# A two-layer encoder in float32: output projections and w_down by token instead of by feature

## Chip, cores and metric

One core of a Trainium2 chip. The metric is device time of one execution in microseconds (us). The kernel before takes 2138.07 us, the median of 3 runs (2137.47 to 2138.16).

## What is computed

256 tokens of 2048 features go through two pre-norm layers, in float32. Layer 0 has chunked attention in 8 heads beside differential attention in 4; layer 1 has an index-selected sparse attention in 16 heads over a shared latent. What matters here is the frame around the heads:

```python
for layer in range(DEPTH):                       # DEPTH = 2
    h = rmsnorm(x, attn_norm[layer])
    p = h @ w_in                                 # even_w_in or odd_w_in
    mix = heads(p) @ w_out                       # even_w_out or odd_w_out, 2048 x 2048
    x = x + mix
    h = rmsnorm(x, ffn_norm[layer])
    x = x + (silu(h @ w_gate[layer]) * (h @ w_up[layer])) @ w_down[layer]   # 5632 x 2048
return rmsnorm(x, final_norm)
```

## The kernel before

**Numbers.** Every large product is made of three: operands are split into a high part in a reduced float32 form (F32R) and a remainder (low), and high x high, high x low and low x high are summed in PSUM. Activations live as `[feature, high/low, token]` tiles: `xs` (normalised input, 16 tiles of 128 features), `mix` (heads' output), `y` (FFN's inner activations, 44 tiles).

**Weights.** All weights are streamed once, in an order that the generator `sources` (L97) sets, in pieces of 256 input features by 512 outputs, laid out as 128 x 1024. `load_w` (L120) issues a piece's DMA on SyncE's queue (SP) into one of 5 buffers `wl`, ScalarE (ACT) writes the high part `wh` and VectorE (DVE) the remainder `wo`, 3 buffers each. `next_w` (L139) keeps up to three pieces loaded ahead in program order.

**Two forms of product.** `gemm_t` (L187) gives outputs by feature: the weight is the stationary operand, 128 outputs at a time, and the tokens stream. Per piece and 128 outputs it issues two matmuls of `wh` with high and low tokens side by side, 512 columns, and two of `wo` with the high tokens, 256 columns; 16 matmuls per piece into four PSUM banks `acc0` to `acc3`, whose two halves still have to be added. `gemm_n` (L222) gives outputs by token: a block of 128 tokens is stationary, and 512 weight columns stream; per piece 12 matmuls of 512 columns into two banks `nat0` and `nat1`. Only value projections and `w_uv` use `gemm_n`; everything else, output projections (`out_proj`, L576) and `w_down` (`ffn_layer`, L617) among it, uses `gemm_t`.

**Order around the change.** Python code issues instructions in program order, and a tile framework places semaphores and buffers. While a product runs, `pump` (L150) advances a queue of generators, `steps`, twice per piece: norm statistics, attention scores and mixes are slipped between matmuls that way. `drain` empties the queue.

**Residual and norms.** The residual `xt` is kept by feature, `[128, 16, 256]`. A product's 512 outputs are one of four groups. After each group `add_residual` (L307) adds both halves of four banks to `xt` (`add_tiles`, 8 adds on DVE), writes the next `xs` with the norm's gain (`normalize_tiles`, ACT and DVE) and squares on ACT (`add_squares`), which GpSimd (POOL) sums in `sqacc`. The norm itself is a factor per token: `norm_steps` (L273) sums `sqacc` over partitions by matmuls with ones (`col_sums`), takes the power -1/2 on POOL (`rstd`), and spreads it over partitions with two more matmuls (`rows_of`); products are scaled after the fact.

**The end.** The last group of the last `w_down` holds two pieces back (`last=2`) and finishes its four tiles one after another (`finish_tile`, L638). Then come the sums over partitions, the power, the row, nine steps of scaling on DVE and nine stores of `out_T` (L813 to L825).

`fp.tile([P, 88])`, and `attention_pools(stack, 8)` and `(stack, 168)`, allocate spacers: unused floats in front of `y` and `mix`.

Of the kernel before, what the change touches and what calls it, by code (L numbers as in the profile page):

```python
# [39 lines left out]
def encoder_kernel(  # L40
    ctx: ExitStack,
    tc: tile.TileContext,
    xT: bass.AP,
    gcols: bass.AP,
# [15 lines left out]
    outT: bass.AP,  # L60
# [10 lines left out]
    xt = const.tile([P, KT, S], F32, name="xt")  # L71
# [11 lines left out]

    OUT0 = [4, 5, 6, 7, 0, 1, 2, 3]
# [11 lines left out]

    def sources():  # L97
        for quad in QUADS:
            for g in even_groups(quad):
                yield from (w_ein[g, k] for k in range(KT // 2))  # L100
        for g in range(4):
            yield from (w_eout[g, k] for k in OUT0)
        yield from ffn_sources(0)
        yield from (w_ox[k] for k in range(KT // 2))
        yield from (w_oi[k] for k in range(KT // 2))
        for quad in range(4):
            yield from (w_oq[quad, k] for k in range(KT // 2) if quad)
            yield w_uk[quad]
            yield w_uv[quad]
# [10 lines left out]
    def load_w(cuts=1, between=None):  # L120
        src = next(stream, None)
        if src is None:
            return
        if before:
# [62 lines left out]
    def gemm_t(act, nk, order=None, last=0, done=None, halves=0):  # L187

        banks = [bank([P, 2, S], f"acc{i}") for i in range(4)]
        order = list(range(nk // 2)) if order is None else order  # L190

        def tile_products(n, i, w, js=(0, 1)):
            cs = [slice(j * 512 + n * P, j * 512 + (n + 1) * P) for j in js]
            products(banks[n], P, w, cs, [act[:, 2 * order[i] + j] for j in js],
                     i == 0 and js[0] == 0, i == len(order) - 1)

        for i in range(len(order) - last):
            w = next_w()
            for js in ((0,), (1,)) if i < halves else ((0, 1),):
                for n in range(4):  # L200
                    tile_products(n, i, w, js)
                    if n % 2 and js[-1]:
                        pump()
        if last:
            ws = [next_w() for _ in range(last)]
            done(3, banks[3], False)
            banks.append(bank([P, 2, S], "acc4"))
            for n in range(4):
                for i, (wh, wo) in enumerate(ws):
                    ii = len(order) - last + i  # L210
                    if n < 3:
                        tile_products(n, ii, (wh, wo))
                    else:
                        for j in range(2):
                            c = slice(j * 512 + n * P, j * 512 + (n + 1) * P)
                            a = act[:, 2 * order[ii] + j]
                            mm3(banks[4][:, 0, :], (wh[:, c], wo[:, c]), (a[:, 0, :], a[:, 1, :]),
                                i == 0 and j == 0, i == last - 1 and j == 1)
                done(n, banks[n if n < 3 else 4], True)
        return banks  # L220

    def gemm_n(lhs, nk):  # L222

        banks = [bank([P, 512], f"nat{i}") for i in range(2)]
        for k2 in range(nk // 2):
            wh, wo = next_w()
            for b in range(2):
                for j in range(2):
                    h, l = lhs(2 * k2 + j)
                    t = slice(b * P, (b + 1) * P)  # L230
                    c = slice(j * 512, (j + 1) * 512)
                    mm3(banks[b], (h[:, t], l[:, t]), (wh[:, c], wo[:, c]),
                        k2 == 0 and j == 0, k2 == nk // 2 - 1 and j == 1)
                pump()
        return banks

    def xpair(kt):
        return xs[:, kt, 0, :], xs[:, kt, 1, :]
# [9 lines left out]
    def rstd(total, n, name):  # L248
        v = small.tile([P, 2], F32, name=name + "v", tag="rv", bufs=3)
        nc.vector.tensor_scalar(out=v, in0=total, scalar1=1.0 / n, scalar2=EPS, op0=ALU.mult, op1=ALU.add)  # L250
        r = small.tile([P, 2], F32, name=name + "r", tag="rc", bufs=4)
        nc.gpsimd.tensor_tensor(out=r, in0=v, in1=mhalf, op=ALU.pow)
        return r

    def col_sums(parts, name):
# [5 lines left out]
        return p[:, 0:2]  # L261

# [21 lines left out]
    def normalize_tiles(t0, n, gi):  # L284

        for t in range(t0, t0 + n):
            g = gc[:, gi * KT + t:gi * KT + t + 1]
            nc.scalar.activation(xs[:, t, 0, :], xt[:, t, :], AF.Copy, scale=g)
            nc.vector.scalar_tensor_tensor(out=xs[:, t, 1, :], in0=xt[:, t, :], scalar=g,
                                           in1=xs[:, t, 0, :].bitcast(F32), op0=ALU.mult, op1=ALU.subtract)  # L290

    def add_squares(st, t0, n):
        sq = small.tile([P, 2, S], F32, name="sq", tag="sq")
        nc.scalar.activation(sq[:, :n, :], xt[:, t0:t0 + n, :], AF.Square)  # L294
        if st["acc"] is None:
            st["acc"] = const.tile([P, 2, S], F32, name="sqacc", tag="sqacc")
            nc.gpsimd.tensor_copy(out=st["acc"], in_=sq)
        else:
            nc.gpsimd.tensor_tensor(out=st["acc"][:, :n, :], in0=st["acc"][:, :n, :], in1=sq[:, :n, :], op=ALU.add)  # L299

    def add_tiles(banks, t0):

        for i, b in enumerate(banks):
            for part in range(2):
                nc.vector.tensor_tensor(out=xt[:, t0 + i, :], in0=b[:, part, :], in1=xt[:, t0 + i, :], op=ALU.add)  # L305

    def add_residual(banks, t0, gi, st):  # L307

        for h in range(0, 4, 2):
            add_tiles(banks[h:h + 2], t0 + h)  # L310
            normalize_tiles(t0 + h, 2, gi)
            add_squares(st, t0 + h, 2)
# [6 lines left out]


    nc.scalar.dma_start(out=xt[:, 0:1, :], in_=xT[:, 0:1, :])
# [12 lines left out]
    def load_x(t, n):  # L334
        if t:
            nc.sync.dma_start(out=xt[:, t:t + n, :], in_=xT[:, t:t + n, :])
        normalize_tiles(t, n, 0)
# [8 lines left out]

    def attention_pools(stack, spacer):
        ap = stack.enter_context(tc.tile_pool(name="attn", bufs=2))
        mixp = stack.enter_context(tc.tile_pool(name="mix", bufs=1))
        mixp.tile([P, spacer], F32, name="spacer")  # L350
        return ap, mixp, mixp.tile([P, KT, 2, S], F32R, name="mix")
# [134 lines left out]
    stack = ExitStack()  # L486
    ap, mixp, mix = attention_pools(stack, 8)
# [45 lines left out]
    n0 = {"acc": None}  # L533

    def stat_steps():
        for t in range(0, KT, 2):
            with tc.issue_after(latest["act"].ins):
                add_squares(n0, t, 2)
            yield
        yield from norm_steps(n0, "n0", scale, 4)  # L540

    steps.append(bias_steps())
    for quad in QUADS:
# [21 lines left out]
        vb = gemm_n(xpair, KT)  # L565
# [10 lines left out]
    def out_proj(mix, order, gi):  # L576
        st = {"acc": None}
        for g in range(4):
            banks = gemm_t(mix, KT, order)
            if g == 0:  # L580
                drain()
            add_residual(banks, 4 * g, gi, st)
# [6 lines left out]
    def ffn(st):  # L589

        with tc.tile_pool(name="ffn", bufs=1) as fp:
            fp.tile([P, 88], F32, name="spacer")
# [22 lines left out]
            yield y  # L615

    def ffn_layer(st, gi, last):  # L617
        out = {"acc": None}
        body = ffn(st)
        y = next(body)  # L620
        for g in range(4):
            fin = last and g == 3
            banks = gemm_t(y, FT, last=2 if fin else 0, done=finish_tile(out) if fin else None)
            if fin:
                pass
            elif last:
                for h in range(0, 4, 2):
                    t = 4 * g + h
                    add_tiles(banks[h:h + 2], t)
                    add_squares(out, t, 2)  # L630
                    times_gain(t, 2)
            else:
                add_residual(banks, 4 * g, gi, out)
# [4 lines left out]
    def finish_tile(out):  # L638
        def done(n, b, fin):

            t = 12 + n
            for part in range(1 if n == 3 and fin else 2):
                nc.vector.tensor_tensor(out=xt[:, t, :], in0=b[:, part, :], in1=xt[:, t, :], op=ALU.add)
            if not fin:
                return
            if n < 3:
                add_squares(out, t, 1)
            else:
                sq = small.tile([P, 2, S], F32, name="sq", tag="sq")
                nc.scalar.activation(sq[:, 0, :], xt[:, t, :], AF.Square)  # L650
                out[n] = sq[:, 0, :]
            if n < 2:
                times_gain(t, 1)
        return done

    def times_gain(t0, n):
        for t in range(t0, t0 + n):
            nc.scalar.activation(xt[:, t, :], xt[:, t, :], AF.Copy, scale=gc[:, 64 + t:65 + t])
# [6 lines left out]
    ap, mixp, mix = attention_pools(stack, 168)  # L665
# [144 lines left out]
    out = ffn_layer(st, 4, True)  # L810


    r = rstd(col_sums([out["acc"][:, 1, :], out["acc"][:, 0, :], out[3]], "n4cs"), D, "n4")  # L813
    p = rows_of(r, "n4p")
    t = 0
    for n in (1, 1, 2, 2, 2, 2, 2, 2, 2):
        if t + n < KT:
# [69 lines left out]
```

## Time and profile before

| | |
|---|---|
| median of 3 runs | 2138.07 us |
| the profiled execution | 2138.02 us |
| its span (first to last instruction) | 2136.2 us |
| PE busy | 2122.6 us, 12280 matmul records |
| DVE, ACT, POOL busy | 1347.7, 1067.7, 231.0 us |
| moved by DMA | 398.92 MB, mean 187 GB/s |

The span is what the profile's views divide up; 1.8 us of the execution lie outside it. PE is TensorE's matmul queue, PEld its weight loads. A matmul's recorded end is modelled and overlaps the next one, so what a matmul costs is read from the distance between starts. float32 matmuls (with `ident` or `ones`) leave two records each, transposes one.

### The profile page before, as it was taken

Reading aid. Unit: us, or ns where it says so; the run is one execution under the profiler, and the core shown is the slowest. Engines: PE = TensorE matmul, PEld = TensorE weight load, DVE = VectorE, ACT = ScalarE, POOL = GpSimd, SP = SyncE. Lnnn points to the kernel's source line nnn. Section 1 sums busy time; section 2 is a strip of 40 time slices with the busy share of each in tenths; the row PEclk is TensorE's granted clock in tenths of the full one; section 3 lists DMA queues with packets and bytes.
Section 4 is the critical chain, followed back from the end, with each engine's and each line's share of the span. In section 5 each row is a group of like instructions: output and inputs, shape, how many; then the busy total and the mean of one; then the engine's idle time right before and its main releaser. Section 6 shows DMA issues by size and latency. Waiting matters only on the chain.

```text
span 2136.2 us, 31865 instructions
## 1 busy us (share of the span) xinstructions
PE 2122.6 (99%) x12280; PEld 1862.8 (87%) x12280; DVE 1347.7 (63%) x1978; ACT 1067.7 (50%) x1575; POOL 231.0 (11%) x232
## 2 busy tenths in 40 slices
PE   9999999999999999999999999999999999999998
PEld 8888888888888888888888888888888888888887
DVE  6665557766666666655547977666666666654444
ACT  6555555545454544444435566454454545444442
POOL 3111001100000000000002242110010000100000
PEclk9999999999999999999999999999999999999999
DMA  8455445555555555555556444655555555555553
GB/s 288 163 179 177 168 168 187 189 195 188 190 193 190 190 194 188 192 192 187 180 185 214 164 160 147 198 188 190 195 188 192 192 189 193 191 189 193 191 190 127
DMA packets 114407, 398.92 MB, mean 187 GB/s; under 512 B 12554, under 2 KB 16718, under 8 KB 114254
## 3 DMA queue, kind: packets, MB, share of 16 engines
q1 hardware_dynamic: 114110, 396.75, 56.0%
q8 instruction: 96, 1.57, 0.3%
q14 instruction: 57, 0.47, 0.1%
q10 hardware_dynamic: 144, 0.13, 0.0%
HBM read 394.70 MB, written 2.14 MB: 186 GB/s over the span
## 4 chain that ended last, share of the span: by engine, by line
PE 95%; DVE 2%; POOL 1%; ACT 1%; issue 1%; DMA 1%; SPq 0%; POOLq 0%; DVEq 0%; ACTq 0%
PE acc L171 86%; PE nat L171 4%; PE x L171 1%; DVE wo L136 1%; DMA xt<-in_xT 1%; POOL sqacc L299 1%; PE uk L171 0%; DVE sc L748 0%; DVE sc L758 0%; ACT wh L135 0%; POOL tm L767 0%; DVE m L757 0%; DVE xt L818 0%; PE c3o L171 0%; DVE qT L318 0%
## 5 line engine op out<-in xcount | busy, mean ns | idle before, releaser
L136 DVE TENSOR_TENSOR wo<-wl,wh 128x1024 fp32r<-128x1024 f32 (+2 forms) x747 | 943.6, 1265 | 727.4 <-ACT wh L135 718.1
L135 ACT ACTIVATE wh<-wl 128x1024 fp32r<-128x1024 f32 (+2 forms) x747 | 785.1, 1051 | 897.1 <-PE acc L171 821.6
L171 PE MATMUL acc<-xs,wh 128*128 128x512 f32 x3648 | 1139.4, 393 | 0.2 <-ACT wh L135 0.2
L171 PEld LDWEIGHTS acc<-xs,wo 128*128 128x128 f32 x3648 | 685.1, 188 | 152.5 <-DVE wo L136 2.0
L171 PE MATMUL acc<-xs,wo 128*128 128x256 f32 x3648 | 722.8, 279 | 1.0 <-DVE wo L136 1.0
L171 PEld LDWEIGHTS acc<-xs,wh 128*128 128x128 f32 x3648 | 554.4, 188 | 3.2 <-ACT wh L135 0.9
L171 PE MATMUL acc<-y,wh 128*128 128x512 f32 x1412 | 437.1, 391 | 0.0
L171 PEld LDWEIGHTS acc<-y,wo 128*128 128x128 f32 x1408 | 264.4, 188 | 58.1
L171 PE MATMUL acc<-y,wo 128*128 128x256 f32 x1408 | 278.3, 279 | 0.0
L171 PEld LDWEIGHTS acc<-y,wh 128*128 128x128 f32 x1412 | 213.8, 188 | 0.0
L171 PE MATMUL acc<-mix,wh 128*128 128x512 f32 x512 | 160.0, 394 | 0.0
L317 ACT ACTIVATE u<-acc 128x256 f32<-128x256 f32 x228 | 86.2, 378 | 60.8 <-PE acc L171 55.8
L171 PEld LDWEIGHTS acc<-mix,wo 128*128 128x128 f32 x512 | 96.1, 188 | 21.3
L171 PE MATMUL acc<-mix,wo 128*128 128x256 f32 x512 | 101.1, 279 | 0.0
L299 POOL TENSOR_TENSOR sqacc<-sqacc,sq 128x512 f32<-128x512 f32 (+1 forms) x36 | 53.4, 1483 | 410.3 <-ACT sq L294 408.2
L171 PE MATMUL nat<-wh,xs 128*128 128x512 f32 x256 | 83.6, 394 | 0.0
L606 POOL TENSOR_TENSOR ga<-ga,n1rs 128x256 f32<-128x256 f32 x44 | 36.6, 843 | 425.4 <-DVE ga L605 411.3
L606 POOL TENSOR_TENSOR ga<-ga,n3rs 128x256 f32<-128x256 f32 x44 | 36.6, 843 | 425.5 <-DVE ga L605 411.2
L171 PEld LDWEIGHTS acc<-mix,wh 128*128 128x128 f32 x512 | 77.7, 188 | 0.2
L171 PEld LDWEIGHTS nat<-wh,xs 128*128 128x128 f32 x256 | 48.0, 187 | 10.8
L305 DVE TENSOR_TENSOR xt<-acc,xt 128x256 f32<-128x256 f32 x120 | 44.6, 418 | 19.1 <-PE acc L171 19.1
L171 PE MATMUL nat<-wo,xs 128*128 128x512 f32 x128 | 50.5, 394 | 0.0
(811 smaller groups left out, 1084.7 us busy)
## 6 DMA issues: line engine op xcount, KB each, us to landing
wl<-in_w_gate SPq DMA_DIRECT2D x176, 512.0 KB, 3.3
wl<-in_w_up SPq DMA_DIRECT2D x176, 512.0 KB, 3.3
wl<-in_w_down SPq DMA_DIRECT2D x176, 512.0 KB, 3.3
wl<-in_w_ein SPq DMA_DIRECT2D x93, 512.0 KB, 3.3
wl<-in_w_eout SPq DMA_DIRECT2D x32, 512.0 KB, 3.3
wl<-in_w_oq SPq DMA_DIRECT2D x32, 512.0 KB, 3.2
wl<-in_w_oout SPq DMA_DIRECT2D x32, 512.0 KB, 3.4
wl<-in_w_oi SPq DMA_DIRECT2D x8, 512.0 KB, 4.3
```

Of the source, the lines that this page charges most:

```text
L135: latest["act"] = nc.scalar.activation(wh[:, c], wl[:, c], AF.Copy)
L136: nc.vector.tensor_tensor(out=wo[:, c], in0=wl[:, c], in1=wh[:, c].bitcast(F32), op=ALU.subtract)
L171: nc.tensor.matmul(out, a, b, start=start, stop=stop, skip_group_check=True)
L299: nc.gpsimd.tensor_tensor(out=st["acc"][:, :n, :], in0=st["acc"][:, :n, :], in1=sq[:, :n, :], op=ALU.add)
L305: nc.vector.tensor_tensor(out=xt[:, t0 + i, :], in0=b[:, part, :], in1=xt[:, t0 + i, :], op=ALU.add)
L317: nc.scalar.activation(u[:m], b[:m, 0, :], AF.Copy)
L606: nc.gpsimd.tensor_tensor(out=a, in0=a, in1=st["rs"], op=ALU.mult)
```

## The change

- `out_proj` and `w_down` use `gemm_n`, which takes an order of pieces and the held-back last pieces; `gemm_t` loses both.
- The residual is kept by token: `xn`, `[128, 2 blocks, 2048]`. `xT` is still read for the first `xs`, and a second copy of the input, `xN`, is loaded into `xn` during the second product (`stat_steps`).
- After a group `add_residual` makes one add per bank and one square with a running sum on ACT (`accum_out`), and queues `transpose_steps`: 8 transposes on PE in two banks, each bank then normalised into `xs` from PSUM, one bank per two pumps.
- Sums over features are a reduction of four numbers per token on DVE (`total`); the ones-matmuls of the layer norms go.
- At the end each token block is finished by itself (`finish_block`): add, square, reduce, power, four scalings on ACT and DVE, four stores of `out_N`. The final gain is loaded as a row spread over partitions (`gf`) and multiplied in on POOL for the earlier groups.
- `wh` and `wo` get 32 more floats per buffer, and value-projection and `w_uv` pieces are written 16 floats further in (`OFF`). Spacers become 16, 16 and 96 floats.

```diff
+    OFF = 16
+    SP0, SP1, SPY = 16, 16, 96
+    UKO, UVO = 0, OFF
+    def moving(pieces):
+        return ((src, OFF) for src in pieces)
...
+            yield from moving(w_ein[v, k] for k in range(KT // 2))
...
-        wh = wpool.tile([P, width], F32R, name="wh", tag="wh", bufs=3)
-        wo = wpool.tile([P, width], F32R, name="wo", tag="wo", bufs=3)
+        wh, wo = (wpool.tile([P, width + 2 * OFF], F32R, name=n, tag=n, bufs=3)[:, off:off + width] for n in ("wh", "wo"))
...
+    def gemm_n(lhs, nk, order=None, last=0, done=None):
+
+        banks = [bank([P, 512], f"nat{i}") for i in range(2)]
+        order = list(range(nk // 2)) if order is None else order
+
+        def block_products(b, i, w):
+            wh, wo = w
+            for j in range(2):
+                h, l = lhs(2 * order[i] + j)
+                t = slice(b * P, (b + 1) * P)
+                c = slice(j * 512, (j + 1) * 512)
+                mm3(banks[b], (h[:, t], l[:, t]), (wh[:, c], wo[:, c]),
+                    i == 0 and j == 0, i == len(order) - 1 and j == 1)
+
+        for i in range(len(order) - last):
+            w = next_w()
+            for b in range(2):
+                block_products(b, i, w)
+                pump()
         if last:
             ws = [next_w() for _ in range(last)]
...
+            for b in range(2):
+                for i, w in enumerate(ws):
+                    block_products(b, len(order) - last + i, w)
+                done(b, banks[b])
         return banks
...
+    def total(sums):
+
+        t = small.tile([P, 2], F32, name="tot", tag="tot", bufs=3)[:, :sums.shape[1]]
+        nc.vector.tensor_reduce(out=t, in_=sums, op=ALU.add, axis=mybir.AxisListType.X)
+        return t
...
-    def norm_steps(st, name, second, wait=6):
+    def norm_steps(st, name, second, wait=2):
         yield from idle(wait)
-        st["r"] = rstd(col_sums([folded(st["acc"])], name + "cs"), D, name)
+        st["r"] = rstd(total(st["sums"]), D, name)
...
+    def add_squares(st, b, g):
+        sq = small.tile([P, 512], F32, name="sq", tag="sq")
+        nc.scalar.activation(sq, xn[:, b, 512 * g:512 * g + 512], AF.Square, accum_out=st["sums"][:, b, g:g + 1])
+
+    def add_block(bk, b, g, st):
+
+        c = xn[:, b, 512 * g:512 * g + 512]
+        nc.vector.tensor_tensor(out=c, in0=bk, in1=c, op=ALU.add)
+        add_squares(st, b, g)
+
+    def transpose_steps(g, gi):
+
+        yield
+        for t in range(4 * g, 4 * g + 4, 2):
+            p = bank([P, 512], f"xT{t}")
+            for i in range(2):
+                for b in range(2):
+                    k = 2 * i + b
+                    nc.tensor.transpose(p[:, k * P:(k + 1) * P], xn[:, b, (t + i) * P:(t + i + 1) * P], ident)
+            yield
+            for i in range(2):
+                normalize(t + i, p[:, i * S:(i + 1) * S], gi)
+            yield
...
     def stat_steps():
-        for t in range(0, KT, 2):
+        for b in range(2):
+            for c in (slice(0, D // 2), slice(D // 2, D)):
+                nc.sync.dma_start(out=xn[:, b, c], in_=xN[:, b, c])
+                yield
+        for g in range(4):
             with tc.issue_after(latest["act"].ins):
-                add_squares(n0, t, 2)
-            yield
-        yield from norm_steps(n0, "n0", scale, 4)
+                for b in range(2):
+                    add_squares(n0, b, g)
+            yield
+        yield from norm_steps(n0, "n0", scale, 1)
...
-            banks = gemm_t(mix, KT, order)
+            banks = gemm_n(pairs(mix), KT, order)
...
+            banks = gemm_n(pairs(y), FT, last=2 if fin else 0, done=partial(finish_block, out, gf) if fin else None)
...
+    def finish_block(out, gf, b, bk):
+
+        add_block(bk, b, 3, out)
+        r = rstd(total(out["sums"][:, b:b + 1, :]), D, f"n4{b}")
+        for g in (0, 1, 2, 3):
+            c = slice(512 * g, 512 * g + 512)
+            x = xn[:, b, c]
+            if g == 3:
+                nc.vector.scalar_tensor_tensor(out=x, in0=x, scalar=r, in1=gf[:, c], op0=ALU.mult, op1=ALU.mult)
+            elif g == 1:
+                nc.vector.tensor_scalar(out=x, in0=x, scalar1=r, scalar2=None, op0=ALU.mult)
             else:
+                nc.scalar.activation(x, x, AF.Copy, scale=r)
+            nc.sync.dma_start(out=outN[:, b, c], in_=x)
```

PE's order, at the first two pieces of a `w_down` group. Before, a piece is these eight rows (an `acc` number is a PSUM bank's tile):

```order
L171 MATMUL acc_8412<-y,wh 128x512 x2
L171 MATMUL acc_8412<-y,wo 128x256 x2
L171 MATMUL acc_8413<-y,wh 128x512 x2
L171 MATMUL acc_8413<-y,wo 128x256 x2
L171 MATMUL acc_8414<-y,wh 128x512 x2
L171 MATMUL acc_8414<-y,wo 128x256 x2
L171 MATMUL acc_8415<-y,wh 128x512 x2
L171 MATMUL acc_8415<-y,wo 128x256 x2
```

Now the second group begins so (`xT` is the bank that the transposes write, `xn` the residual by token):

```order
L181 MATMUL nat_9104<-wh,y 128x512
L181 MATMUL nat_9104<-wo,y 128x512
L181 MATMUL nat_9104<-wh,y 128x512 x2
L181 MATMUL nat_9104<-wo,y 128x512
L181 MATMUL nat_9104<-wh,y 128x512
L181 MATMUL nat_9105<-wh,y 128x512
L181 MATMUL nat_9105<-wo,y 128x512
L181 MATMUL nat_9105<-wh,y 128x512 x2
L181 MATMUL nat_9105<-wo,y 128x512
L181 MATMUL nat_9105<-wh,y 128x512
L323 MATMUL xT_9124<-ident,xn 128x128 x4
```

Sixteen matmuls in two widths have become twelve in one, six for each token block, and four transposes of the group before stand behind the first piece (four more behind the second).

DVE's order at the end of the program. Before, after the last weight piece:

```order
L643 TENSOR_TENSOR xt<-acc_19535,xt 128x256 x2
L643 TENSOR_TENSOR xt<-acc_19532,xt 128x256 x2
L643 TENSOR_TENSOR xt<-acc_19533,xt 128x256 x2
L643 TENSOR_TENSOR xt<-acc_19534,xt 128x256 x2
L643 TENSOR_TENSOR xt<-acc_19978,xt 128x256
L250 TENSOR_SCALAR n4v<-n4cs 128x2
L818 TENSOR_TENSOR xt<-xt,n4p 128x256 x2
L818 TENSOR_TENSOR xt<-xt,n4p 128x512 x6
L822 SCALAR_TENSOR_TENSOR xt<-xt,gc,n4p 128x256 x2
```

Now (`tot` is the sum of squares, `n40r` and `n41r` the blocks' factors, `gf` the final gain):

```order
L312 TENSOR_TENSOR xn<-nat_18615,xn 128x512
L271 TENSOR_REDUCE tot<-sums 128x1
L255 TENSOR_SCALAR n40v<-tot 128x1
L676 TENSOR_SCALAR xn<-xn,n40r 128x512
L674 SCALAR_TENSOR_TENSOR xn<-xn,n40r,gf 128x512
L312 TENSOR_TENSOR xn<-nat_18616,xn 128x512
L271 TENSOR_REDUCE tot<-sums 128x1
L255 TENSOR_SCALAR n41v<-tot 128x1
L676 TENSOR_SCALAR xn<-xn,n41r 128x512
L674 SCALAR_TENSOR_TENSOR xn<-xn,n41r,gf 128x512
```

One scaling of everything at the end has become two, and the second block's add stands behind the first block's scalings.

SP's order of loads in the second product now (`fa`, `ft` and `hk` belong to the bias tables; before, the same rows stand without the three of `xn`, and with four weight pieces ahead of the second):

```order
L144 DMA wl<-in_w_ein 128x1024 x3
L561 DMA xn<-in_xN 128x1024
L532 DMA frows<-ft 20x384
L561 DMA xn<-in_xN 128x1024
L144 DMA wl<-in_w_ein 128x1024
L543 DMA hk<-frows 128x4x256
L561 DMA xn<-in_xN 128x1024 x2
L144 DMA wl<-in_w_ein 128x1024 x7
```

Four loads of 512 KB stand among the weight pieces.

## Rows read from the trace of the kernel before

**Rows 1.** The page: span, busy time by engine, tenths in 40 slices.

```profile
span 2136.2 us, 31865 instructions
...
PE 2122.6 (99%) x12280; PEld 1862.8 (87%) x12280; DVE 1347.7 (63%) x1978; ACT 1067.7 (50%) x1575; POOL 231.0 (11%) x232
...
PEclk9999999999999999999999999999999999999999
DMA  8455445555555555555556444655555555555553
```

**Rows 2.** The page: the chain that ended last, by line.

```profile
PE acc L171 86%; PE nat L171 4%; PE x L171 1%; DVE wo L136 1%; DMA xt<-in_xT 1%; POOL sqacc L299 1%; PE uk L171 0%; DVE sc L748 0%; DVE sc L758 0%; ACT wh L135 0%; POOL tm L767 0%; DVE m L757 0%; DVE xt L818 0%; PE c3o L171 0%; DVE qT L318 0%
```

**Rows 3.** The same chain in order of time: start us, us, what.

```profile
129.13 6.99 PE nat L171 x30
...
405.66 716.22 PE acc L171 x4152
...
1262.51 2.80 PE nat L171 x12
...
1320.75 82.83 PE acc L171 x480
```

**Rows 4.** Timeline of PE, two products: start us, us, engine, line, operation.

```profile
129.66 0.39 PE L171 MATMUL nat<-wh,xs 128*128 128x512 f32 x1
129.89 0.40 PE L171 MATMUL nat<-wo,xs 128*128 128x512 f32 x1
...
420.00 0.62 PE L171 MATMUL acc<-xs,wh 128*128 128x512 f32 x2
420.46 0.39 PE L171 MATMUL acc<-xs,wo 128*128 128x256 f32 x2
420.68 0.62 PE L171 MATMUL acc<-xs,wh 128*128 128x512 f32 x2
```

**Rows 5.** Timeline of PE around three transposes in the attention stage.

```profile
81.25 0.49 PE L377 MATMUL b20pt<-ident,b200lg 128*128 128x128 f32 x3
81.50 0.71 PE L171 MATMUL acc<-xs,wh 128*128 128x512 f32 x2
82.04 0.40 PE L171 MATMUL acc<-xs,wo 128*128 128x256 f32 x2
```

**Rows 6.** Timeline of PE around a set of ones-matmuls.

```profile
401.84 0.50 PE L171 MATMUL n1cs<-ones,sqacc 128*128 128x1 f32 x4
402.20 0.71 PE L171 MATMUL acc<-xs,wh 128*128 128x512 f32 x2
402.75 0.40 PE L171 MATMUL acc<-xs,wo 128*128 128x256 f32 x2
```

**Rows 7.** Busy time in two stretches; last three: PE clock, DMA share, GB/s.

```profile
31.00:55.00 24.00, 23.77 (x140) 20.81 (x140) 16.41 (x17) 15.12 (x23) 16.55 (x13) 1.00 0.76 255
405.66:600.00 194.34, 194.34 (x1129) 171.04 (x1128) 126.76 (x179) 97.78 (x144) 15.88 (x19) 1.00 0.58 191
```

**Rows 8.** Durations by line, ns min/median/max: squares, residual adds.

```profile
L294 ACT ACTIVATE sq<-xt x41: 417/617/636, 32.8 to 2123.1; 128x512 f32<-128x512 f32 x38, 128x256 f32<-128x256 f32 x3
...
L305 DVE TENSOR_TENSOR xt<-acc,xt x120: 410/418/425, 324.1 to 2065.3; 128x256 f32<-128x256 f32 x120
```

**Rows 9.** Timeline of the end, all engines.

```profile
2123.20 0.28 PE L171 MATMUL acc<-y,wo 128*128 128x256 f32 x1
...
2123.51 0.42 DVE L643 TENSOR_TENSOR xt<-acc,xt 128x256 f32<-128x256 f32 x1 [0.48 <-PE acc L171]
...
2125.56 0.16 DVE L250 TENSOR_SCALAR n4v<-n4cs 128x2 f32<-128x2 f32 x1 [1.62 <-PE n4cs L171]
2125.80 0.70 POOL L252 TENSOR_TENSOR n4r<-n4v,mhalf 128x2 f32<-128x2 f32 x1 [1.38 <-DVE n4v L250]
...
2128.26 5.03 SPq L824 DMA_DIRECT2D out_T<-xt  x9
2132.06 0.87 DVE L822 SCALAR_TENSOR_TENSOR xt<-xt,gc,n4p 128x256 f32<-128x256 f32 x2
```

More of the change, by code (lines that the diff above doesn't have):

```diff
@@ L220, in gemm_t @@
-        return banks
[L222 to L235, printed above, removed]
@@ L282, in bc2 @@
         return t[:, None, :].to_broadcast([P, 2, S])
[L284 to L312, printed above, removed]
+    def normalize(t, src, gi):
+        g = gc[:, gi * KT + t:gi * KT + t + 1]
+        nc.scalar.activation(xs[:, t, 0, :], src, AF.Copy, scale=g)
+        nc.vector.scalar_tensor_tensor(out=xs[:, t, 1, :], in0=src, scalar=g,
+                                       in1=xs[:, t, 0, :].bitcast(F32), op0=ALU.mult, op1=ALU.subtract)
@@ new lines, in new_sums @@
+    def new_sums():
+        return {"sums": small.tile([P, 2, 4], F32, name="sums", tag="sums", bufs=2)}
+    def add_squares(st, b, g):
[17 more added lines that the diff above has]
+            yield
@@ L314, in combined, with add_residual @@
+    def add_residual(banks, g, gi, st):
+        for b in range(2):
+            add_block(banks[b], b, g, st)
+        steps.append(transpose_steps(g, gi))
     def combined(dst, b, m=P):
@@ L614, in ffn @@
                     split((y[:, t, 0, :], y[:, t, 1, :]), a)
-            yield y
+            yield y, fp
     def ffn_layer(st, gi, last):
-        out = {"acc": None}
+        out = new_sums()
         body = ffn(st)
-        y = next(body)
+        y, fp = next(body)
+        if last:
+            gf = fp.tile([P, D], F32, name="gf", tag="ga", bufs=1)
+            nc.sync.dma_start(out=gf, in_=bass.AP(tensor=gfin.tensor, offset=gfin.offset, ap=[[0, P], [1, D]]))
         for g in range(4):
             fin = last and g == 3
[L623 to L633, printed above, removed]
+            banks = gemm_n(pairs(y), FT, last=2 if fin else 0, done=partial(finish_block, out, gf) if fin else None)
+            if not last:
+                add_residual(banks, g, gi, out)
+            elif not fin:
+                for b in range(2):
+                    add_block(banks[b], b, g, out)
+                    c = slice(512 * g, 512 * g + 512)
+                    nc.gpsimd.tensor_tensor(out=xn[:, b, c], in0=xn[:, b, c], in1=gf[:, c], op=ALU.mult)
         for _ in body:
@@ L636, in ffn_layer @@
         return out
[L638 to L647, printed above, removed]
-            else:
[L649 to L658, printed above, removed]
+    def finish_block(out, gf, b, bk):
+        add_block(bk, b, 3, out)
+        r = rstd(total(out["sums"][:, b:b + 1, :]), D, f"n4{b}")
+        for g in (0, 1, 2, 3):
+            c = slice(512 * g, 512 * g + 512)
+            x = xn[:, b, c]
[3 more added lines that the diff above has]
+                nc.vector.tensor_scalar(out=x, in0=x, scalar1=r, scalar2=None, op0=ALU.mult)
+            else:
+                nc.scalar.activation(x, x, AF.Copy, scale=r)
+            nc.sync.dma_start(out=outN[:, b, c], in_=x)
     steps.append(norm_steps(st, "n1", 0.5))
```

104 lines of the change are left out of this document (44 added, 60 removed).

## The prediction

> **What bounds the kernel now.** [...] The chain in order of time then shows stretches in which PE never waits: 4152 matmuls in 716.22 us, 480 in 82.83 us [rows 3]. The profiled execution took 2138.02 us, so 1.8 us lie around its span; the median of the runs, 2138.07 us, is the same number, and I make the sum against 2138.0. What a measurement of this kernel can tell from no change is about 0.2%, 4.3 us.
>
> So the time is a count of PE work. A piece of weights is 256 by 512, and is worth 6144 streamed columns in either form: 8 matmuls of 512 columns and 8 of 256 in `gemm_t`, 12 of 512 in `gemm_n`. The stretches give 716.22 / 4152 x 16 = 2.760 us per piece for `gemm_t`, and 82.83 / 480 x 16 = 2.761 in the stretch that has the second output projection. The natural form is in the trace as well: 30 matmuls in 6.99 us, 2.796 us per piece, and 12 in 2.80 us with the latent tile `c` as the other operand [rows 3]. The timeline shows why: two 512-wide `acc` matmuls start 0.46 us before the 256-wide ones behind them, which take 0.22 us for two, while `nat` matmuls start 0.23 us apart each [rows 4]. Fewer instructions don't buy anything here: per column the natural form is the slower one.
>
> **The change part by part.** *Products.* 32 pieces of `w_eout`, 32 of `w_oout` and 176 of `w_down` go from the one form to the other: 240 x (2.796 - 2.760) = +8.6 us, all on the path, since PE has no gap in these stretches.
>
> *Placement.* The new kernel moves operands in SBUF: value projections and `w_uv` are loaded 16 floats (64 bytes) further into their tile, and spacers put `mix` and `y` 64 bytes off from where they were. In the built program streamed and stationary operand of the natural products then lie equal modulo 128 bytes; in the `nat` rows with `xs` they lie 64 bytes apart. The `nat` row with `c` is one where they already lie equal, and it shows 2.80 us for 12 [rows 3]. So I take no gain, for the 36 natural pieces that exist nor for the 240 new ones. The bound below: if each ran at the shortest spacing of two 512-wide matmuls in sight (0.46 / 2 = 0.23, and single `acc` spacings a little under it), see the first rivals. The bound above is the 2.80 of that row, +1 us.
>
> *Transposes.* 3 residuals x 4 groups x 2 banks x 4 = 96 PE transposes of 128 x 128. Three such transposes hold the next matmul back from 81.25 to 81.50, and the next pair of 512 takes 0.54 instead of 0.46 [rows 5]: 0.33 us for three, 0.11 us each. 96 x 0.11 = +10.6 us. They come between matmuls of a PE that is never idle, so nothing hides them. [...]
>
> *Column sums.* Sums of squares now come from ACT's accumulator and a small DVE reduction, so PE loses four sets of ones-matmuls inside the stages. One set holds the next matmul from 401.84 to 402.20 and stretches the pair behind it to 0.55 [rows 6]: 0.45 us. 4 x 0.45 = -1.8 us.
>
> *DVE, ACT and POOL at a group's end.* Removed per group: 8 adds of 0.418 us, four normalisations straight from `xt`, two squares of 0.617 us, and POOL's accumulation [rows 8]. Added: two adds of 512 columns, two squares, four normalisations a little later from PSUM. I cost this at nothing: between 405.66 and 600 us DVE is busy 65% and ACT 50% of a stretch in which PE has no idle time [rows 7], and the change takes work away. Where it could fail: ACT squares both blocks only after DVE's adds, and the weight conversion of the piece three ahead stands behind them. The adds end about 1 us after the group's last matmul, the squares 0.8 us later, the conversion 1.05 and DVE's subtraction 1.25 us after that: about 4 us, and PE has two converted pieces, 5.5 us, in hand. The first transposes stand after a full piece (2.8 us) of the next product, so they don't wait for the adds either. If that cover were gone, each of 12 boundaries would cost some tenths of a us.
>
> *Start.* Four loads of 512 KB of `xn` enter SP's queue among the first weight pieces. The core moves 255 GB/s between 31 and 55 us, DMA engines are 76% busy, PE idles 0.23 us of 24 [rows 7]. 2 MB more are about 8 us of transfers at that rate, taken from five buffered pieces of lead. Behind them in SP's queue stand weight pieces 11 and 12 and the bias table; on ACT four squares of 0.62 us are now in a row ahead of a weight conversion, twice. I put this at 0, with bounds of -1 (the column sums' wait there goes) and +4 us (half the transfer time appears). The 1 MB row of gains for the last norm is loaded during `w_down`, where DMA engines are busy 5 tenths [rows 1]: 0.
>
> *End.* Before, 13.0 us pass between the start of the last matmul at 2123.20 and the span's end at 2136.2: adds, squares, POOL sum, ones-matmuls, power, a row broadcast, then nine steps of scaling with the stores behind them; the last scaling ends at 2132.93, and the last store 3.3 us later, with the span [rows 9]. After: matmul to add 0.4, add 0.7 (two of 0.42 at most), square 0.65, reduction and scaling 0.32, power 0.70, four quarter-rows on two engines 1.3, store 3.3, and about 0.4 us between engines: 7.8 us. But on DVE the second block's add stands behind the first block's two scalings, which wait for the first block's power. That block ends 2.8 us earlier and needs about 4.7 us to there, so the add starts 1.9 us after the last matmul's start, not 0.4: 9.3 us in all. 9.3 - 13.0 = -3.7 us (bounds -5 and -2).
>
> **Sum:** +8.6 + 10.6 - 1.8 + 0 - 3.7 = +13.7 us, which makes 2151.7; I take 2151, because the bounds at the start and the end lean downwards a little. Its own range is 2146 to 2157.
>
> **The rivals.** *First, the other sign: placement makes natural matmuls fast.* The place is every natural matmul; the mechanism is that streamed and stationary reads disturb each other less when the operands lie differently. For it: the same columns take 2.760 or 2.796 us per piece in this trace, so something other than columns has a price, and the change shifts just these operands. Against it: the row with `c`, at the new relation, is no faster [rows 3]. If a 512-wide matmul went down to 0.226 us, a piece would be 2.712: 240 x (2.712 - 2.760) = -11.5, the 36 old natural pieces 36 x (2.712 - 2.796) = -3.0, the rest +5.1: -9.4, 2128.6 us. It decides from 0.229 us per matmul on, where pieces pay for the transposes.
>
> *Second, equal price per column.* Natural matmuls fall to the 0.23 us of the 512-wide `acc` pair [rows 4], 2.76 us per piece. Then products cost 0, the old natural pieces give -1.3, and the rest is +5.1: +3.8, 2141.8 us, at the edge of no difference. [...]
>
> *Third, transposes at their full duration.* If each cost the 0.27 us that a record lasts (0.49 us for three that start 0.11 us apart) [rows 5] because PE drains around a group, 96 x 0.27 = 25.9 instead of 10.6: +29, 2167 us. Against it: the next matmul starts 0.25 us after the first of three.
>
> **How the numbers follow.** The forecast gets 0.56, the first rival 0.27, the second 0.12, the third 0.05. The range reaches from 2127, just under the first rival's value, to 2158, the top of the forecast's own range; it leaves out the third rival and the first one's faster half. Faster by over 0.2%: the first rival and a little of the second, 0.29. Within: the rest of the second that falls there, 0.10. Slower: 0.61.
>
> **What would show it.** Stretches of `nat` with `y` in the chain should read 2.79 to 2.80 us for 12 matmuls; under 2.75 proves the first rival. Groups of four transposes should hold the next matmul back about 0.35 us with the pair behind them 0.08 longer, and no PE idle time should be put down to DVE or ACT at the 12 boundaries. From the last matmul's start to the end it should be 8 to 11 us. DVE's total should fall by some 20 us (96 adds of 0.42 against 24 of about 0.7) without effect. I am wrong if a stretch of `w_down` shows PE waiting for a weight piece, or if the `acc` stretches, which the change leaves alone, no longer read 2.760.

## The result, and the profile after

The changed kernel takes 2161.93 us, the median of 4 runs (2161.70 to 2162.52), against 2137.77 for the kernel before on the same chip: a ratio of 1.0114, 95% interval 1.0096 to 1.0131. It is slower, as forecast, but by 24 us where 13 were forecast, and beyond the top of the range. The profiled execution took 2161.7 us.

The page of the kernel after: span, busy time by engine, granted clock, and the chain that ended last by line (the answer to [rows 1, 2]):

```profile
span 2159.9 us, 29908 instructions
...
PE 2148.4 (99%) x11380; PEld 1836.1 (85%) x11380; DVE 1299.2 (60%) x1882; ACT 1065.6 (49%) x1603; POOL 178.6 (8%) x194
...
PEclk9999999999999999999999999999999999999999
...
PE acc L181 59%; PE nat L181 35%; PE x L181 1%; PE uk L181 1%; DMA xt<-in_xT 1%; PE xT L323 0%; PE is L181 0%; PE c3o L181 0%; PE a0o L181 0%; PE a1o L181 0%; PE c2o L181 0%; PE c0o L181 0%; PE c1o L181 0%; DVE wo L146 0%; PE b31o L181 0%
```

PE has 900 matmul records fewer and is busy 26 us longer; the granted clock reads 9 in all 40 slices (0.999 over the execution), and PE is still the whole chain. So the time is again a count of PE work, and the chain in order of time tells which work has changed (start us, us, what; compare [rows 3]):

```profile
202.65 6.90 PE nat L181 x30
...
332.33 19.43 PE nat L181 x84
...
410.50 479.55 PE acc L181 x2736
890.05 63.83 PE nat L181 x276
...
1372.26 19.36 PE nat L181 x84
...
1427.21 479.56 PE acc L181 x2736
1906.77 241.39 PE nat L181 x1044
```

A gate or up piece, 16 matmuls of `gemm_t` that the change left alone, now takes 479.55 / 2736 x 16 = 2.804 us where it took 2.760 [rows 3]. For the 342 pieces of these two stretches that is 15.2 us. The pieces that did change form were cheaper than forecast: 241.39 / 1044 x 12 = 2.775 us for `w_down`, 2.77 to 2.78 for the output projections, not 2.796.

The other terms came out nearly as put. The first of the two groups of four transposes at the first boundary of `w_down` (timeline of PE; start us, us):

```profile
953.48 0.40 PE L181 MATMUL nat<-wh,y 128*128 128x512 f32 x1
953.72 0.60 PE L323 MATMUL xT<-ident,xn 128*128 128x128 f32 x4
954.08 0.48 PE L181 MATMUL nat<-wh,y 128*128 128x512 f32 x1
954.40 0.40 PE L181 MATMUL nat<-wo,y 128*128 128x512 f32 x1
```

It holds the next matmul for 0.36 us, and that one holds its successor for 0.32 instead of 0.23: 0.45 us for four. All 24 groups of this trace hold the next matmul for 0.35 to 0.36 us, so they make 24 x 0.45 = 10.8 us. The start (busy time in a stretch, last three columns PE clock, DMA share, GB/s, as in [rows 7]) and all of PE's waits in the kernel after (who waits, for what; us in total, times, longest):

```profile
31.00:55.00 24.00, 24.00 (x139) 21.04 (x138) 13.57 (x19) 16.09 (x34) 3.54 (x5) 1.00 0.91 316
```

```profile
PE warm L181 <- POOL ident masks.py:199: 1.4, 1, 1.4
PE acc L181 <- DVE wo L146: 0.5, 1, 0.5
PE acc L181 <- ACT wh L145: 0.5, 1, 0.5
```

The core simply moves 316 GB/s there, where 255 had been enough, so the 2 MB of `xn` are hidden; piece 17 (`nat`) starts at 54.54 in the chain of the kernel after. No boundary makes PE wait for DVE's adds or ACT's squares. The end (all engines):

```profile
2150.53 0.40 PE L181 MATMUL nat<-wh,y 128*128 128x512 f32 x1
...
2151.74 0.69 DVE L312 TENSOR_TENSOR xn<-nat,xn 128x512 f32<-128x512 f32 x1
...
2154.23 1.33 ACT L678 ACTIVATE xn<-xn,n41r 128x512 f32<-128x512 f32 x2 [1.05 <-POOL n41r L257]
```

From the last matmul's start to the span's end it is 2159.9 - 2150.53 = 9.4 us, forecast 9.3.

### The profile page after: what moved, and what is told of

Same layout as the page of the kernel before. It is cut to its first block, busy times and chain, and to the rows that moved or that the text cites. A ratio compares the mean times of both kernels' runs of the same rounds, so it can differ in the third digit from the quotient of the medians.

```text
span 2159.9 us, 29908 instructions
## 1 busy us (share of the span) xinstructions
PE 2148.4 (99%) x11380; PEld 1836.1 (85%) x11380; DVE 1299.2 (60%) x1882; ACT 1065.6 (49%) x1603; POOL 178.6 (8%) x194
## 4 chain that ended last, share of the span: by engine, by line
PE 98%; DMA 1%; DVE 0%; ACT 0%; issue 0%; SPq 0%; ACTq 0%; POOLq 0%; POOL 0%
PE acc L181 59%; PE nat L181 35%; PE x L181 1%; PE uk L181 1%; DMA xt<-in_xT 1%; PE xT L323 0%; PE is L181 0%; PE c3o L181 0%; PE a0o L181 0%; PE a1o L181 0%; PE c2o L181 0%; PE c0o L181 0%; PE c1o L181 0%; DVE wo L146 0%; PE b31o L181 0%
## 5 line engine op out<-in xcount | busy, mean ns | idle before, releaser
L181 PE MATMUL nat<-wh,y 128*128 128x512 f32 x1408 | 441.6, 394 | 0.0
L181 PEld LDWEIGHTS nat<-wh,y 128*128 128x128 f32 x1408 | 264.2, 188 | 61.4
L181 PE MATMUL nat<-wo,y 128*128 128x512 f32 x704 | 276.4, 393 | 0.0
L181 PE MATMUL nat<-wh,mix 128*128 128x512 f32 x512 | 166.7, 397 | 0.0
L181 PEld LDWEIGHTS nat<-wo,y 128*128 128x128 f32 x704 | 132.3, 188 | 29.8
L181 PEld LDWEIGHTS nat<-wh,mix 128*128 128x128 f32 x512 | 96.1, 188 | 21.1
L181 PE MATMUL nat<-wo,mix 128*128 128x512 f32 x256 | 100.4, 392 | 0.0
L181 PEld LDWEIGHTS nat<-wo,mix 128*128 128x128 f32 x256 | 48.2, 188 | 9.7
L298 ACT ACTIVATE xs<-xT,gc 128x256 fp32r<-128x256 f32 x48 | 22.4, 467 | 31.0 <-DVE xs L299 31.0
L632 ACT ACTIVATE th<-ga 128x256 f32<-128x256 f32 x88 | 33.8, 410 | 5.8 <-DVE ga L630 5.7
```

The costliest lines, as they stand in the source:

```text
L181: nc.tensor.matmul(out, a, b, start=start, stop=stop, skip_group_check=True)
L298: nc.scalar.activation(xs[:, t, 0, :], src, AF.Copy, scale=g)
L632: nc.scalar.activation(th, a, AF.Tanh, scale=0.5)
```

## The experiments

The question: why do products that the change doesn't touch cost 1.6% more? Nothing in their code differs but where their operands lie. A *natural* piece below is one of `gemm_n`, a *transposed* piece one of `gemm_t`; neither has to do with the transposes on PE. In the programs as built, every `wh` and `wo` buffer of the kernel before begins at 64 bytes modulo 256 (they are 4096 bytes apart), and `xs` at 128. The change pads each buffer by `2 * OFF` = 32 floats, 128 bytes, so the three buffers of a ring begin at 64, 192 and 64 bytes (`wh`) and 192, 64, 192 (`wo`). Theory P: the padding is the cause. Below, *distance* is the streamed operand's address minus the stationary one's, modulo 256 bytes. Rival T: PE's finer mixture of transposes and natural products disturbs the stretches behind it, wherever the buffers lie.

**e1, no padding.** The change with `OFF` 0; value pieces lose their shift too.

```diff
-    OFF = 16
+    OFF = 0
```

> The changed kernel with OFF = 0: the weight buffers wh and wo are again 1024 floats each, one behind the other, and value-projection pieces start at their tile's beginning; nothing else differs. Theory P (placement): the untouched gemm_t products got slower, 2.804 us per piece (2736 matmuls in 479.55 us) where they had 2.760, because 32 more floats per buffer put every second buffer 128 bytes off modulo 256. Then the gate and up stretches read 2.760 again and 456 pieces give back 0.044 us each: 2162 - 20 = 2142 us. Theory T (traffic): they got slower by something else that the change brings (transposes between matmuls, reads of PSUM, other DMA). Then the time stays at 2162 and the stretches at 2.80.

Measured: 2134.83 us (10 runs), ratio 0.9988, interval 0.9978 to 0.9997. The chain in order of time:

```profile
331.12 19.09 PE nat L181 x84
...
408.19 471.97 PE acc L181 x2736
...
1334.37 19.59 PE nat L181 x84
...
1884.85 236.68 PE nat L181 x1044
```

`acc` is back at 2.760 us. P had put 2142 us, without a gain of the natural pieces. These split: `w_down` (distance 0 to `y`) takes 2.720 us, 0.2267 per matmul, `w_eout` (distance 0) 2.727, `w_oout`, whose `mix` lies 128 bytes off, 2.799. That is the price of my first rival, and it sorts by the distance modulo 256, not 128.

**e2, the padding alone, in the kernel before.** No natural product is added, no transpose.

```diff
-        wh = wpool.tile([P, width], F32R, name="wh", tag="wh", bufs=3)
-        wo = wpool.tile([P, width], F32R, name="wo", tag="wo", bufs=3)
+        wh, wo = (wpool.tile([P, width + 32], F32R, name=n, tag=n, bufs=3)[:, :width] for n in ("wh", "wo"))
...
-    ap, mixp, mix = attention_pools(stack, 168)
+    ap, mixp, mix = attention_pools(stack, 104)
```

> The kernel before with 32 more floats in each wh and wo buffer, unused (the second spacer is 64 floats smaller to make room, which leaves mix where it was modulo 256). Theory P: all 697 gemm_t pieces go from 2.760 to about 2.80 us: 2138 + 31 = 2169 us. Theory T: no change, 2138 us.

Measured: 2165.01 us (4 runs), ratio 1.0128, interval 1.0113 to 1.0143. The chain, and starts of the first matmul of four successive pieces in the timeline:

```profile
407.64 727.76 PE acc L170 x4152
...
1422.53 726.30 PE acc L170 x4144
```

```profile
551.91 0.63 PE L170 MATMUL acc<-xs,wh 128*128 128x512 f32 x2
...
554.72 0.63 PE L170 MATMUL acc<-xs,wh 128*128 128x512 f32 x2
...
557.51 0.62 PE L170 MATMUL acc<-xs,wh 128*128 128x512 f32 x2
...
560.32 0.63 PE L170 MATMUL acc<-xs,wh 128*128 128x512 f32 x2
```

727.76 / 4152 x 16 = 2.804 us a piece, the number of the kernel after; single pieces take 2.81, 2.79, 2.81 as the buffers alternate. The padding by itself costs 27 to 28 us, where P had put 31. T falls.

**e3, a padding that keeps the alignment.** The change with 64 floats, 256 bytes, in place of 32, all else kept.

```diff
-        wh, wo = (wpool.tile([P, width + 2 * OFF], F32R, name=n, tag=n, bufs=3)[:, off:off + width] for n in ("wh", "wo"))
+        wh, wo = (wpool.tile([P, width + 4 * OFF], F32R, name=n, tag=n, bufs=3)[:, off:off + width] for n in ("wh", "wo"))
```

> The changed kernel with 64 more floats per wh and wo buffer in place of 32, so that the buffers lie 4352 bytes apart (17 x 256) and keep the 16-float shift of the value pieces. If the offset modulo 256 bytes is what counts: gemm_t at 2.760, 2142 us. If it is any distance other than 4096 (a larger modulus): gemm_t stays at 2.79 to 2.81, 2160 us. Theory T: 2162 us.

Measured: 2133.40 us (10 runs), ratio 0.9981, interval 0.9972 to 0.9990; `acc` 471.97 us for 2736 as in e1. So it isn't that there is a padding: 256 bytes leave `acc` at 2.760 us, as none do, and 128 make it 2.804.

**e4, no transposes.** As e1, but the transposes and their banks are left out, and `xs` is made from untransposed values, so its products are of other numbers.

```diff
-            p = bank([P, 512], f"xT{t}")
-            for i in range(2):
-                for b in range(2):
-                    k = 2 * i + b
-                    nc.tensor.transpose(p[:, k * P:(k + 1) * P], xn[:, b, (t + i) * P:(t + i + 1) * P], ident)
...
-                normalize(t + i, p[:, i * S:(i + 1) * S], gi)
+                normalize(t + i, xn[:, i, 512 * g:512 * g + S], gi)
```

> As e1, with the 96 transposes and their PSUM banks left out: xs is normalised straight from xn, so what the later products multiply is not the transposed residual. Forecast's price: 96 x 0.11 = 10.6 us less than e1, 2131 us if e1 has 2142. If a transpose costs its whole record of 0.27 us, or slows the matmuls behind it: 26 us or more less, 2116 us.

Measured: 2123.01 us (one run), 11.8 under e1: 0.12 us for each of 96, with what they disturb. Forecast 10.6.

**e5, one offset for each family of pieces.** On e3; theory E is that buffers need only be alike.

```diff
-            yield from (w_gate[layer, g, k] for k in range(KT // 2))
-            yield from (w_up[layer, g, k] for k in range(KT // 2))
+            yield from ((w_gate[layer, g, k], (32, 48)[layer]) for k in range(KT // 2))
+            yield from ((w_up[layer, g, k], (16, 0)[layer]) for k in range(KT // 2))
...
-            yield from (w_down[layer, g, k] for k in range(FT // 2))
+            yield from ((w_down[layer, g, k], (16, 32)[layer]) for k in range(FT // 2))
...
-            yield from (w_eout[g, k] for k in OUT0)
+            yield from ((w_eout[g, k], 48) for k in OUT0)
```

> As the 64-float padding (stride 4352 bytes, a multiple of 256), but each family of pieces gets its own offset, the same in all its buffers: gate and up of layer 0 stand 192 and 0 bytes from their streamed operand (modulo 256), gate and up of layer 1 128 and 64, w_down of layer 0 64, w_down of layer 1 128, w_eout 192. Theory P (the distance between streamed and stationary operand modulo 256 bytes sets a matmul's time): the families differ. Up of layer 1 stays at 2.760 us a piece, up of layer 0 (distance 0) takes 2.720, gate of layer 1 and w_down of layer 1 (distance 128) about 2.79 to 2.80, w_down of layer 0 (distance 64) 2.760, w_eout (distance 192) 2.80. Theory E (what counts is only that all buffers of a ring lie alike, whatever the distance): gate and up stay at 2.760 in both layers and w_down at 2.720 wherever they stand.

Measured: 2150.05 us (one run). Layer 0 and 1 in the chain:

```profile
353.66 19.60 PE nat L181 x84
...
408.94 475.56 PE acc L181 x2736
884.51 63.19 PE nat L181 x276
...
1419.27 474.61 PE acc L181 x2736
1893.88 242.62 PE nat L181 x1044
```

E falls: natural pieces take 2.747 us at distance 64 (63.19 / 276 x 12), 2.789 at 128, 2.800 at 192. P's guess for transposed pieces falls too: between starts of successive pieces in the timeline, `acc` takes 2.787 us at distances 0 and 128, 2.760 at 64, 2.773 at 192, once a group has settled. Of the distances tried the two forms have their best in different places: natural pieces at 0 (2.720 us, e1), transposed ones at 64 (2.760).

**e6 and e7, the best distances.** On e3, `mix` of layer 1 moves by 128 bytes (e6); then gate, up and `w_uk` pieces also move by 64 bytes (e7).

```diff
-    SP0, SP1, SPY = 16, 16, 96
+    SP0, SP1, SPY = 16, 48, 96
```

> As the 64-float padding, with layer 1's mix moved by 128 bytes, so that all four natural projections stand at distance 0 from their weights, and c moved with it. Theory P: w_oout's 32 pieces go from 2.80 to 2.720 us, 2.6 us in all: 2130.8 us, ratio 0.997. Theory E: nothing, 2133.4.

Measured for e6: 2131.61 us (7 runs), ratio 0.9972, interval 0.9961 to 0.9983. `w_oout`'s stretches of 84 go from 19.59 us in e3 to 19.09 in e6. Of what these products read, only the stationary `mix` had moved, long since written; weights, buffers and the writes into them stood where they were. (The other tiles of `mix`'s pool moved with it, but these products don't read them.)

```profile
1332.71 19.59 PE nat L181 x84
```

```profile
1332.33 19.09 PE nat L181 x84
```

> As the run before, and the gate, up and uk pieces moved by 64 bytes, so that nearly every product of both layers' FFN stands at distance 0 too. Theory P: the acc products of both FFN go from 2.760 to 2.720 us a piece, 342 pieces, 13.7 us: about 2117 us, ratio 0.990. Theory E: nothing, as the run before. A third possibility, that transposed and natural products differ for another reason than the distance (three-dimensional output, the PSUM banks), also gives 2.760 for them.

Measured for e7: 2140.68 us (11 runs), ratio 1.0015, interval 1.0006 to 1.0024. The forecast of 2117 was wrong, in sign against e6: 476.53 / 2736 x 16 = 2.787 us.

```profile
406.45 476.53 PE acc L181 x2736
```

**e8, `wh` and `wo` of a piece 128 bytes apart.** On e6, with an offset for each.

```diff
-        wh, wo = (wpool.tile([P, width + 4 * OFF], F32R, name=n, tag=n, bufs=3)[:, off:off + width] for n in ("wh", "wo"))
+        offs = off if isinstance(off, tuple) else (off, off)
+        wh, wo = (wpool.tile([P, width + 4 * OFF], F32R, name=n, tag=n, bufs=3)[:, o:o + width] for n, o in zip(("wh", "wo"), offs))
```

> As e6, but hi and lo halves of a piece (wh and wo) lie 128 bytes apart, in the same way in every buffer of a family: (wh 64, wo 192) for gate and up of layer 0, gate of layer 1 and w_down of layer 0; (wh 192, wo 64) for up and w_down of layer 1. Theory A (each matmul pays by its own distance alone): a transposed piece then costs between the 2.760 us of distance 64 and the 2.775 that the offset table gives for 192, so FFN stretches of about 2.77 us a piece. Theory B (what the padding broke is that wh and wo of one piece lie differently): the stretches of layer 0 go to 2.81 us a piece with wh at 64 and wo at 192, and those of layer 1 to about 2.80, although all buffers of the ring lie alike. Theory C (it takes buffers that alternate from one piece to the next): as A, 2.77.

Measured: 2146.66 us (one run). The starts of two pieces four apart, in layer 0 and in layer 1, both with `wh` at 64 and `wo` at 192, and between them the fourth and the seventh piece of layer 1's first gate group, which have the same places:

```profile
550.32 0.62 PE L182 MATMUL acc<-xs,wh 128*128 128x512 f32 x2
...
561.41 0.62 PE L182 MATMUL acc<-xs,wh 128*128 128x512 f32 x2
...
1410.35 0.63 PE L182 MATMUL acc<-xs,wh 128*128 128x512 f32 x2
...
1413.17 0.63 PE L182 MATMUL acc<-xs,wh 128*128 128x512 f32 x2
...
1415.98 0.61 PE L182 MATMUL n3p<-ident,n3r 128*128 128x128 f32 x4
...
1419.19 0.62 PE L182 MATMUL acc<-xs,wh 128*128 128x512 f32 x2
...
1421.96 0.62 PE L182 MATMUL acc<-xs,wh 128*128 128x512 f32 x2
...
1500.07 0.63 PE L182 MATMUL acc<-xs,wh 128*128 128x512 f32 x2
...
1511.32 0.63 PE L182 MATMUL acc<-xs,wh 128*128 128x512 f32 x2
```

The same pieces with the same places take 11.09 / 4 = 2.773 us in layer 0 and 11.25 / 4 = 2.813 in layer 1, where up pieces with the two places exchanged come between. A group of eight keeps the dear price, 2.81 us for the last of the four pieces too (1508.51 to 1511.32), long after the last exchanged piece. The layer is not what decides: the fourth piece of layer 1's first gate group takes 2.82 us, and the seventh 2.77, behind the small matmuls of the norm (`n3p`), before any exchanged piece has run; layer 0 shows the same (8.44 us for three pieces, 2.81 each, from 397.39 in the chain, and 2.773 later). So none of A, B and C alone is right: such a stretch shows two steady prices, 2.773 and 2.813 us, and which one it takes goes with what ran before. 2.813, with 2.792 and 2.809 for the first pieces behind an exchange and behind the exchange back, are also the prices of the alternating buffers in e2.

**e9, finer distances.** On e6, gate, up and `w_down` at distances of 32, 96 and 224.

> As e6, with distances between the multiples of 64 bytes: gate of layer 0 at 32, up of layer 0 at 96, gate of layer 1 at 224 (modulo 256), w_down of layer 0 at 32, w_down of layer 1 at 224. If the price changes smoothly with the distance, transposed pieces at 32 and 96 lie between the neighbours: 2.76 to 2.79 us a piece, and natural ones at 32 and 224 between 2.720 and 2.747 or 2.80. If it goes by steps of 64 bytes, 32 equals 0 or 64 in both kinds. Should a transposed piece come under 2.760, an arrangement better than e6 exists.

Measured: 2158.21 us (one run). No step and no slope: `acc` takes 2.827 us at 32, 2.800 at 96, 2.812 at 224, each above both neighbours (2.760 to 2.787 in e5), and `w_down` 2.80 at both:

```profile
406.15 480.93 PE acc L181 x2736
887.08 64.38 PE nat L181 x276
...
1901.10 243.60 PE nat L181 x1044
```

**e10, all pairs of places.**

```diff
+    PAIRS = [(16 * (i % 4), 16 * (i // 4 % 4)) for i in range(2 * (FT // 4))]
...
-            yield from (w_gate[layer, g, k] for k in range(KT // 2))
+            yield from ((w_gate[layer, g, k], PAIRS[(FT // 4) * layer + g]) for k in range(KT // 2))
```

> As e6, but the gate pieces of each successive group of the two FFN take another pair of places for wh and wo, all sixteen pairs of 64, 128, 192 and 0 bytes (modulo 256) in turn, the first six of them a second time; the up pieces between them stay at 64 and 64. If each matmul's own distance makes its price, up stays at 2.760 us a piece everywhere, and a gate piece costs what its two halves cost in the offset table (2.760 to 2.79). If the price also hangs on what ran before, as the split run shows for (64, 192), then up pieces, which never change, differ between groups, by some 0.01 to 0.05 us. A pair that comes under 2.760 would point to an arrangement better than e6.

Measured: 2138.63 us (one run). A gate piece, once settled, between starts in the timeline, us:

| `wo` \ `wh` at | 64 | 128 | 192 | 0 |
|---|---|---|---|---|
| 64 | 2.760 | 2.773 | 2.773 | 2.820 |
| 128 | 2.800 | 2.787 | 2.853 | 2.827 |
| 192 | 2.813 | 2.800 | 2.773 | 2.827 |
| 0 | 2.800 | 2.800 | 2.800 | 2.787 |

Two rows of the pair (192, 128), four pieces apart, the start of its last but one piece, and the starts of the first three of the unchanged up pieces behind it:

```profile
662.24 0.63 PE L183 MATMUL acc<-xs,wh 128*128 128x512 f32 x2
...
673.65 0.63 PE L183 MATMUL acc<-xs,wh 128*128 128x512 f32 x2
...
676.50 0.64 PE L183 MATMUL acc<-xs,wh 128*128 128x512 f32 x2
...
682.21 0.63 PE L183 MATMUL acc<-xs,wh 128*128 128x512 f32 x2
...
685.00 0.62 PE L183 MATMUL acc<-xs,wh 128*128 128x512 f32 x2
...
687.76 0.62 PE L183 MATMUL acc<-xs,wh 128*128 128x512 f32 x2
```

11.41 / 4 = 2.853 us against 2.76. The price follows the pieces that PE reads and not those that ACT and DVE write meanwhile: beside the last two gate pieces the first two up pieces are being written (with three buffers, a finished piece's buffer takes the third piece behind it), and the two gate pieces still take (682.21 - 676.50) / 2 = 2.855 us. Up pieces pay up to 0.04 us in the first piece behind some changes of place (here 685.00 - 682.21 = 2.79 us) and are at 2.760 from the second on. Where `wh` and `wo` lie differently the price is not the mean of their own (192 and 128 alone: 2.773 and 2.787). No pair comes under 2.760; the place that the kernel before has by chance is the best of the sixteen, and e6 is the fastest version seen that computes the same.

## Why the prediction was right in sign and wrong in size

The sign was right by luck. With the padding made harmless and all else kept (e3) the change is 0.19% faster, 2133.40 us: the first rival's gain of the natural pieces outweighs the transposes. What made the kernel slower is a term that the forecast didn't have.

- **The step that failed** is the first one, that the time is a count of pieces whose prices move with their form alone: *Products* took the 2.760 us of `gemm_t` as fixed, and *Placement* weighed the moved operands only for natural pieces. The padding of `wh` and `wo` was in the diff and got no term. It took `acc` from 2.760 to 2.804 us: 15.2 us in the two long stretches of the FFN, and by the same price up to 5 more in the other 114 of 456 `acc` pieces. The sign that the prediction named for itself, `acc` stretches off 2.760, is what appeared.
- **Products**: +8.6 forecast. The 240 pieces cost 176 x (2.775 - 2.760) + 64 x about 0.011 = +3.3 us, with natural pieces of distances 0 and 128 mixed by the same padding (unpadded, in e1, `w_down` takes 2.720); the old natural pieces gave -1.3 (6.90 for 6.99).
- **Placement**: the gain was refused because the `c` row, with operands equal modulo 128, showed 2.80 [rows 3]. In bytes that pair is at 192 and 64: equal modulo 128, but 128 apart modulo 256, the place that costs 2.799 us in e1. At distance 0 a natural matmul takes 0.2267 us (e1, e3, e6), within 0.001 us of the first rival's 0.226. The gain was real, though no run shows that it comes from reads that disturb each other less; its counter-evidence was read with the wrong modulus. By the prices of distance 0 e6 should be 2138.0 + 240 x (2.720 - 2.760) - 36 x (2.796 - 2.728) + 10.8 - 1.8 - 0.8 - 3.6 = 2130.6 us; it measured 2131.6.
- **Transposes**: +10.6 forecast, 10.8 by the timeline, 11.8 by e4. The third rival's drain would have been 26 us and is excluded.
- **Start**: 0 forecast, -0.8 measured by when piece 17 starts in the two chains (54.54, and 55.31 before); the loads hide.
- **End**: -3.7 forecast, 9.4 - 13.0 = -3.6. Within it two errors cancel: the last add starts 1.2 us after the matmul, not 1.9, and from the last scaling to the span's end it is 2159.9 - 2155.56 = 4.3 us, not 3.3.
- **Column sums**: -1.8 forecast; the four sets are gone from the trace, but no run prices them alone.
- **DVE, ACT, POOL at the boundaries**: 0 forecast; PE waits for none. DVE's total fell by 48.5 us, not by some 20, and without effect, as put.

The sum of these terms, 15.2 + 5 + 3.3 - 1.3 + 10.8 - 1.8 - 0.8 - 3.6, is 26.8; the profiled executions differ by 23.7, so it is 3 us too high. Part of that is in the 5: from the first `w_ox` matmul to the first of `w_oout`, in the attention of layer 1, e2 takes 177.57 us (1135.24 to 1312.81) where the kernel before takes 177.19 (1121.72 to 1298.91), 0.4 more, though its 40 `acc` pieces would add 1.8 by the price of the long stretches. Why they add less stays open. And the -0.8 at the start has one of the four sets of column sums, 0.45 us, in it a second time. The rest stays unassigned.

What stays open is what the distance acts on. e6 against e3 shows for natural pieces that it is TensorE's own operands, since only an already written stationary tile moved and `w_oout` went from 2.799 to 2.727 us; for transposed pieces e10 shows that it is the pieces being read (2.855 us for the last two gate pieces while up pieces are written), but no run moves `xs`, so that there too the distance counts, and not the weights' place alone, is not shown. e8 shows that a stretch has more than one steady price (2.773 and 2.813 us). What makes the place of an operand cost time, no run here shows.

## What to carry to other kernels

A padding or spacer moves every buffer behind it. Here a ring whose buffers lie 4224 bytes apart took transposed pieces to 2.804 us (e2), where 4096 and 4352 bytes, both multiples of 256, left them at 2.760 (e1, e3), and a stationary tile moved by 128 bytes took natural pieces from 2.799 to 2.727 (e3, e6). So compare the built addresses modulo 256 bytes of streamed and stationary operands before and after, for the products that the change leaves alone too, and give a ring's buffers a stride that is a multiple of 256. When PE is the bound, read the price of a product per place, from starts in stretches without waits, and find each form's best place by giving families of pieces different offsets within one run. Here such a repair of one constant, with one spacer, turned 1.1% slower into 0.28% faster.

## What was not expected of the hardware

- Natural matmuls of 512 columns in F32R cost 0.2267 us at distance 0 between operands (e1, e3, e6), 0.229 at 64 (e5), 0.232 to 0.233 at 128 (e5, e1) and 0.233 at 192 (e5), at an unchanged clock (0.999 granted in the profiled executions of e1, e3, e5, e6 and e10); a transposed piece 2.760 to 2.853 us by the places of its two halves (e10).
- The best distance of those tried differs by form: 0 for 512 streamed weight columns (2.720 us, e1), 64 for tokens streamed past weights (2.760 in e6, where 0 costs 2.787 in e7).
- The price hung on what ran before: 2.773 or 2.813 us for the same pieces in the same places, and 2.77 behind the small matmuls of the norm where it had been 2.82 ahead of them (e8).
- The core moved 316 GB/s from 31 to 55 us of the kernel after, beside a PE that was busy for all 24.00 us.
